# A hybrid decoder trunk: narrower kernel matrices in the recurrent branch, a new planned order, and a third fp32 weight tile per light chunk

## The chip, the cores and the metric

The kernel runs on one core of a Trainium2 chip. The metric is the device time of one execution in microseconds; three runs are taken and their median is compared. Beside them stands one profiled execution, whose trace gives every duration below.

## The reference, cut to what matters

256 tokens of width 1024 pass two layers. In each, one normalised input feeds sliding-window attention (8 query heads, 2 key heads) and a recurrent branch; both are normalised and go through one output matrix. Layer 0 ends in a dense gated block of width 3584, layer 1 in a mixture of 8 experts of the same width with the best 2 per token.

```
bb = f * b                                   # per group of 16 channels, 64 complex states
s  = associative_scan(a, einsum('blgc,gnc->blgn', u, bb))
y  = einsum(s_re, c_re) - einsum(s_im, c_im) + d_skip * u
y  = gelu(y);  y = y * sigmoid(y @ w_glu)
x  = x + mix @ w_o
x  = x + (silu(h @ wg) * (h @ wu)) @ wd      # dense, or top 2 of 8 experts
```

All arrays are float32.

## The kernel before

**Numbers.** A float32 weight tile of 128 x 1024 is loaded (`w`, 512 KB) and split into a rounded part `wh` (ScalarE) and the rest `wl` (VectorE), both float32r; the activation is split in the same way. A product takes three float32r matmuls (`mm3`: wh by xh, wl by xh, wh by xl), or one float32 matmul where a tile is used whole. Float32 matmuls show as two records each in the trace.

**Stages.** `mixer(0)`, `dense`, `mixer(1)`, `moe`. The dense block has 7 chunks of 512 hidden columns, 12 tiles each (4 gate, 4 up, 4 down), for two blocks of 128 tokens. The experts are sorted by the number of their rows and taken in the order of `TURNS`, a heavy one (up to 128 rows, places 0 to 3) and a light one (up to 64 rows, places 4 to 7) in turn, 7 chunks of 12 tiles each. A heavy chunk makes three matmuls per half tile. In a light chunk the stationary block holds the 64 high and the 64 low parts side by side, so that a half tile takes two matmuls (`both`), and the two halves of the result are added by a small matmul with `fold` after a copy `low` (`join`). A tile whose number is in `ENTIRE` isn't split: one float32 matmul per half tile reads it as it landed. That is tile 7, the last of the up half, in each of the 28 light chunks.

**The recurrent branch.** Four time steps are taken together. `prep` makes the input matrices G, the rotations E and the decay. `prep_out` makes the output matrices: H (`HB`, with zeros between the two groups of channels that share the partitions) and T, the direct path within four steps, from products of `BB` with `CB`, `DD` and `HB`. `ssm` runs two halves of 8 groups: input products into two banks, six VectorE instructions, two scans, the rotation back into `sr` and `si` (shifted by one step), then per group three products of 128 columns (with T, and with H for the real and the imaginary part), gelu, a turn, and the gated matrix.

**The order.** All instructions are recorded first. `Plan.order` simulates the five engines with its own cost of each instruction (`cost`), its own delay between engines (`lag`) and the number of buffers (44 of 4 KB per partition, 8 small ones, 8 banks), and always starts the ready instruction with the highest priority: its path to the end plus the entry of its stage in `BONUS`. Each engine then has its instructions in that order, as does SyncE's queue for the loads. The buffers are handed out in that order too: a load waits in SyncE's queue until the buffer that it takes has been read. `prep(1)` and `prep_out(1)` are recorded behind the dense block and may start after its first chunks.

Of the kernel before, what the change touches and what calls it, by code (L numbers as in the profile page):

```python
# [13 lines left out]
AF = mybir.ActivationFunctionType  # L14
# [15 lines left out]
TURNS = (0, 4, 1, 5, 2, 6, 3, 7)  # L30
GROUPS = {0: (0,), 1: (1,), 2: (2, 3), 4: LIGHT}

ENTIRE = (7,)
HEADS = [0, 4, 1, 5, 2, 6, 3, 7]
EPS = 1e-6
BIG = 1e30
# [111 lines left out]


class Plan:  # L150
    between, rate = 0.0027, 360e3

    def __init__(self):
        Plan.between, Plan.rate = 0.0027, 360e3
# [55 lines left out]
    @staticmethod  # L210
    def cost(eng, method, a, k):
        size = lambda v: int(np.prod(v.shape[1:]))
        if method == "registers":
            return 0.5
        if eng == "DMA":
            return int(np.prod(a[0].shape)) * 4 / Plan.rate + 0.01
        n = max(size(v) for v in a if isinstance(v, View))
        if eng == "PE":
            if method == "transpose":
                return 2 * size(a[2]) / 2400 + 0.001  # L220
            if a[2].buf.dtype == F32R:
# [226 lines left out]
class Kernel:  # L448
    NM = 44
    NH = 8  # L450
    gate_at = 6
    BONUS = {'qkv1': -5, 'att0': 43, 'att0s': 29, 'prep0': 5, 'us1': -15, 'xt0': 8, 'ssm1y': -83, 'ssm0g': 60, 'u0': -47, 'wo01': 87, 'qkv0': 2, 'hn': -49, 'route': -33, 'wo011': 54, 'att1s': -26, 'prepo1': -82, 'moe': -5, 'route1': -2, 'att0v': 10, 'rs': -22, 'wo11': 8, 'ssm0': 3, 'route0': 42, 'ssm1': 5, 'wo010': -5, 'att1v': 40, 'xt1': 12, 'us0': 5, 'gates': 5, 'prep1': 15, 'ssm1g': 20, 'att1': 2, 'wo10': 2, 'wo110': -2, 'u1': -2}
    QF = (0, 0)
    HOLD = (1, 2)
    LEAN = (14, 7)
# [344 lines left out]
    def prep_out(self, R):  # L800
# [5 lines left out]
        cr = R["bc"][:, 512:768].rearrange("p (g c) -> p g c", g=16)  # L806
        ci = R["bc"][:, 768:].rearrange("p (g c) -> p g c", g=16)
        dsk = P[0:32, 48:64]
        HB = [[self.M(f"HB{q}{g}") for g in range(2)] for q in range(2)]
        CB = self.M("CB").rearrange("p (r g h c) -> p r g h c", r=2, g=16, h=2)  # L810
        BB = self.M("BB").rearrange("p (r g h c) -> p r g h c", r=2, g=16, h=2)
        T = [self.M(f"T{g}") for g in range(2)]
        for t in HB[0] + HB[1] + T:
            nc.gpsimd.memset(t, 0.0)
        nc.gpsimd.memset(CB, 0.0)
        nc.gpsimd.memset(BB, 0.0)
        for h in range(2):
            ps = slice(64 * h, 64 * h + 64)
            act(CB[ps, 0, :, h, :], cr[ps], AF.Copy)
            act(CB[ps, 1, :, h, :], ci[ps], AF.Copy, scale=-1.0)  # L820
            for q in range(2):
                act(BB[ps, q, :, h, :], Gn[q][ps, :, 3, :], AF.Copy)
        pr = pf[:, 0].unsqueeze(3).to_broadcast([128, 16, 4, 16])
        pi = pf[:, 1].unsqueeze(3).to_broadcast([128, 16, 4, 16])
        c0 = cr.unsqueeze(2).to_broadcast([128, 16, 4, 16])
        c1 = ci.unsqueeze(2).to_broadcast([128, 16, 4, 16])
        for q, (x0, x1) in enumerate(((c0, c1), (c1, c0))):
# [7 lines left out]
            for g in range(2):  # L835
                v = HB[q][g].rearrange("p (g j h c) -> p g j h c", g=8, j=4, h=2)
                for h in range(2):
                    ps = slice(64 * h, 64 * h + 64)
                    act(v[ps, :, :, h, :], w0[ps, 8 * g:8 * g + 8], AF.Copy)
        R["H"] = HB  # L840
        DD = self.H("DD")[0:32].rearrange("p (g c) -> p g c", g=16)
        tt(DD, self.ident[0:32, 0:32].unsqueeze(1).to_broadcast([32, 16, 32]),
           dsk.unsqueeze(2).to_broadcast([32, 16, 32]), OP.mult)
        for b in range(4):
            bank = self.bank()
            g, i0 = b // 2, 4 * (b % 2)
            for k in range(4):
                gp = 4 * b + k
                o = (i0 + k) * 128
                c = k * 128  # L850
                l0, l1, r0, r1 = (x[:, q, gp].rearrange("p h c -> p (h c)") for x in (BB, CB) for q in range(2))
# [6 lines left out]
            src = bank[0:32].rearrange("p (k m) -> p k m", k=4)  # L858
            dst = T[g].rearrange("p (k m) -> p k m", k=8)
            for j in range(4):  # L860
                x, y = dst[32 * j:32 * j + 32, i0:i0 + 4, 32 * j:128], src[:, :, 0:128 - 32 * j]
                if j == 3:
                    nc.vector.tensor_copy(x, y)
                else:
                    act(x, y, AF.Copy)
        R["T"] = T


    def ssm(self, R, X, src, whole):
# [4 lines left out]
        for h in range(2):  # L874
# [9 lines left out]
            (a0, a1), (b0, b1), (sr, si) = (self.two(n) for n in ("sa", "sb", "s"))  # L884
            tt(a0, ec, zr, OP.mult)
            tt(b0, es, zi, OP.mult)
            tt(a0, a0, b0, OP.add)
# [7 lines left out]
            for x in (sr, si):  # L895
                nc.clear(x.rearrange("p (g k) -> p g k", g=8)[:, :, 0:1])
            tt(a0, ec, b0, OP.mult)
            tt(a1, es, b1, OP.mult)
            tt(late(sr), soon(a0), soon(a1), OP.subtract)
            tt(a0, ec, b1, OP.mult)  # L900
            tt(a1, es, b0, OP.mult)
# [5 lines left out]
            for b in range(2):  # L907
                Y = self.bank()
                for i in range(4):
# [5 lines left out]
                    nc.tensor.matmul(y, X[:, gp * 64:(gp + 1) * 64], R["T"][h][:, w], start=True, stop=False)  # L915
                    nc.tensor.matmul(y, sr[:, m], R["H"][0][h][:, w], start=False, stop=False)
                    nc.tensor.matmul(y, si[:, m], R["H"][1][h][:, w], start=False, stop=True)
                act(Yg[0:64, 512 * b:512 * b + 512].rearrange("p (j g c) -> p g j c", j=4, g=4),
                    Y[0:64, :].rearrange("p (g j c) -> p g j c", g=4, j=4), AF.Gelu_apprx_tanh)
# [810 lines left out]
```

## Time and profile before

| | |
|---|---|
| median of 3 runs (lowest to highest) | 1419.39 us (1418.64 to 1421.01) |
| profiled execution, its span | 1417.69 us, 1415.9 us |
| mean granted TensorE clock | 0.993 of 2.4 GHz |
| busy: TensorE, weight loads, VectorE, ScalarE | 1374.0, 1073.1, 1204.1, 998.9 us |
| read from memory | 420.10 MB, of it 672 tiles of 512 KB of the experts |

Busy times are shares of engines, not of the path: matmuls are pipelined and the end of each is modelled, so a TensorE that is always busy may still pause for fractions of a microsecond. The distance from one start to the next tells what an instruction costs in a row of its like. Windows give the busy time of each engine in a stretch, the granted clock, and the share and rate of the DMA engines.

### The profile page before, as it was taken

How to read it: one execution, taken by the hardware profiler on the slowest of the kernel's cores; microseconds unless marked ns; L12 is line 12 of the kernel's file. 1: busy time of each engine (PE TensorE's matmuls, PEld its weight loads, DVE VectorE, ACT ScalarE, POOL GpSimd, SP SyncE). 2: the span in 40 equal slices, each digit the busy share in tenths (PEclk: the TensorE clock that was granted, in tenths of full speed). 3: DMA queues.
4: the chain of work that ended last, by engine and by line, in shares of the span. 5: the costliest groups of instructions: out<-in, count | busy, mean ns of one | idle time of the engine just before them, and what ended most of it. 6: DMA issues, size and time to landing. Idle time of an engine off the chain costs nothing.

```text
span 1415.9 us, 20663 instructions
## 1 busy us (share of the span) xinstructions
PE 1374.0 (97%) x6550; PEld 1073.1 (76%) x6550; DVE 1204.1 (85%) x1642; ACT 998.9 (71%) x1314; POOL 25.5 (2%) x44
## 2 busy tenths in 40 slices
PE   7999999999999999999999999999999999999996
PEld 4888888888888878877678876778887667887654
DVE  8889985554685699999989889989989999998987
ACT  5486754444527387799787788878779778787775
POOL 3000110000000000000000000000000000000000
PEclk9999999999999999999999999999999999999999
DMA  6357155555546759689999999999999999999993
GB/s 220 101 172 252 46 161 177 192 193 162 168 141 240 296 192 360 251 334 397 359 375 371 394 388 406 395 352 370 390 387 393 395 408 372 385 381 400 409 408 146
DMA packets 116899, 422.57 MB, mean 298 GB/s; under 512 B 13360, under 2 KB 13872, under 8 KB 116784
## 3 DMA queue, kind: packets, MB, share of 16 engines
q1 hardware_dynamic: 116784, 421.20, 79.5%
q8 instruction: 53, 0.87, 0.2%
q14 instruction: 62, 0.51, 0.1%
HBM read 420.10 MB, written 1.05 MB: 297 GB/s over the span
## 4 chain that ended last, share of the span: by engine, by line
PE 85%; DVE 6%; DMA 3%; issue 3%; ACT 2%; SPq 0%; DVEq 0%; ACTq 0%
PE bank L445 85%; DVE wl L445 4%; DMA w<-in_moe_dram 3%; ACT wh L445 2%; DMA w<-in_win_u_dram 1%; DVE X L445 1%; ACT st L445 0%; SPq L445 0%; DVE ht L445 0%; DVE htl L445 0%; ACT xh L445 0%; DVE psm L445 0%; DVE xl L445 0%; ACT L445 0%; DVE yl L445 0%
## 5 line engine op out<-in xcount | busy, mean ns | idle before, releaser
L445 DVE TENSOR_TENSOR wl<-w,wh 128x1024 fp32r<-128x1024 f32 x758 | 882.7, 1215 | 86.8 <-ACT wh L445 54.2
L445 ACT ACTIVATE wh<-w 128x1024 fp32r<-128x1024 f32 x758 | 749.3, 1052 | 80.3 <-DMA w<-in_dense_dram 29.5
L445 PE MATMUL bank<-wh,xh 128*128 128x512 f32 x448 | 174.8, 396 | 2.8 <-DVE ht L445 1.9
L445 PE MATMUL bank<-wl,xh 128*128 128x512 f32 x448 | 171.7, 394 | 0.8 <-DVE wl L445 0.8
L445 PE MATMUL bank<-wh,xl 128*128 128x512 f32 x448 | 171.5, 393 | 0.1
L445 PE MATMUL bank<-wl,lx 128*128 128x512 f32 x392 | 159.0, 407 | 8.3 <-DVE wl L445 7.9
L445 PE MATMUL bank<-wh,lx 128*128 128x512 f32 x392 | 152.4, 398 | 8.6 <-DVE ht L445 4.7
L445 PE MATMUL bank<-wh,hth 128*128 128x512 f32 x336 | 115.5, 399 | 0.0
L445 PE MATMUL bank<-wh,htl 128*128 128x512 f32 x336 | 114.5, 399 | 0.0
L445 PE MATMUL bank<-wl,hth 128*128 128x512 f32 x336 | 114.4, 396 | 0.0
L445 PEld LDWEIGHTS bank<-wl,lx 128*128 128x128 f32 x392 | 74.5, 190 | 41.8 <-DVE wl L445 26.6
L445 PEld LDWEIGHTS bank<-wh,xh 128*128 128x128 f32 x448 | 84.0, 188 | 22.0 <-ACT wh L445 2.9
L445 PEld LDWEIGHTS bank<-wl,xh 128*128 128x128 f32 x448 | 84.4, 188 | 20.8 <-DVE wl L445 3.2
L445 PEld LDWEIGHTS bank<-wh,xl 128*128 128x128 f32 x448 | 84.0, 189 | 17.7 <-DVE xl L445 0.5
L445 PEld LDWEIGHTS bank<-wh,lx 128*128 128x128 f32 x392 | 74.3, 190 | 26.3 <-ACT wh L445 6.5
L445 PE MATMUL bank<-wh,hh 128*128 128x512 f32 (+1 forms) x288 | 91.5, 385 | 0.4
L445 PE MATMUL bank<-wl,hh 128*128 128x512 f32 (+1 forms) x288 | 90.1, 381 | 0.0
L445 PE MATMUL bank<-wh,hl 128*128 128x512 f32 (+1 forms) x288 | 90.0, 380 | 0.0
L445 PE MATMUL bank<-wh,ht 128*128 128x512 f32 x224 | 89.0, 431 | 0.6 <-ACT wh L445 0.6
L445 PE MATMUL bank<-wl,ht 128*128 128x512 f32 x224 | 84.6, 406 | 2.0 <-DVE wl L445 2.0
L445 PEld LDWEIGHTS bank<-wh,htl 128*128 128x128 f32 x336 | 62.8, 188 | 14.4 <-issue 1.2
L445 PEld LDWEIGHTS bank<-wh,hth 128*128 128x128 f32 x336 | 62.5, 188 | 14.0 <-issue 0.5
(308 smaller groups left out, 1732.1 us busy)
## 6 DMA issues: line engine op xcount, KB each, us to landing
w<-in_moe_dram SPq DMA_DIRECT2D x672, 512.0 KB, 6.3
w<-in_dense_dram SPq DMA_DIRECT2D x84, 512.0 KB, 4.3
w<-in_wo_dram SPq DMA_DIRECT2D x16, 512.0 KB, 4.4
w<-in_win_u_dram SPq DMA_DIRECT2D x8, 512.0 KB, 5.1
w<-in_win_q_dram SPq DMA_DIRECT2D x8, 512.0 KB, 7.6
w<-in_win_kv_dram SPq DMA_DIRECT2D x4, 512.0 KB, 3.6
w<-in_wglu_dram SPq DMA_DIRECT2D x4, 512.0 KB, 3.6
X<-in_x_dram SPq DMA_DIRECT2D x2, 512.0 KB, 4.2
```

The lines of the kernel that those rows point to most:

```text
L445: getattr(engines[o["eng"]], o["method"])(*map(real, o["a"]), **{n: real(v) for n, v in o["k"].items()})
```

## The change

It has three parts. First, the matrices of the recurrent branch lose their zero blocks: the products that make T have 16 and 48 columns in place of 32 and 96, D is added by VectorE, the two channels of a pair are put apart by a factor per partition (`hm`) in the copy into T, and `ssm` keeps the state of each group with its real part above its imaginary part, so that two products of 64 columns take the place of two of 128. Second, the planner's costs, delay and bonuses are other numbers; bonuses may now also be given by stage and engine. Third, tile 3, the last of the gate half, is used whole in light chunks as tile 7 is.

```
-ENTIRE = (7,)
+ENTIRE = (3, 7)
...
 class Plan:
-    between, rate = 0.0027, 360e3
+    between, rate = 0.0135, 360e3
...
         if eng == "ACT":
-            return 0.05 + n * 0.000876 + (0.06 if any(isinstance(v, View) for v in k.values()) else 0)
+            more = 0.1 if any(isinstance(v, View) for v in k.values()) and a[1].buf.kind != "ps" else 0
+            return 0.05 + n * 0.000876 + more + (0.09 if "accum_out" in k else 0)
...
+        if method == "tensor_tensor_scan":
+            return 0.07 + n * 0.00204
...
-        return 0.0 if e == f == "PE" else LAT[e] + (0.13 if f == "PE" and e != "DMA" else 0.0)
+        return 0.0 if e == f == "PE" else LAT[e] + (0.03 if f == "PE" and e != "DMA" else 0.0)
...
-            prio[i] += self.bonus.get(o["tag"], 0.0)
+            prio[i] += self.bonus.get(o["tag"], 0.0) + self.bonus.get(f"{o['tag']}/{o['eng']}", 0.0)
...
-        HB = [[self.M(f"HB{q}{g}") for g in range(2)] for q in range(2)]
-        CB = self.M("CB").rearrange("p (r g h c) -> p r g h c", r=2, g=16, h=2)
+        HS = [self.M(f"HS{b}") for b in range(2)]
...
-        for t in HB[0] + HB[1] + T:
+        for t in T:
             nc.gpsimd.memset(t, 0.0)
-        nc.gpsimd.memset(CB, 0.0)
...
-            act(CB[ps, 0, :, h, :], cr[ps], AF.Copy)
-            act(CB[ps, 1, :, h, :], ci[ps], AF.Copy, scale=-1.0)
...
+        nc.vector.tensor_reduce(hm, eye, AX.X, OP.add)
+        tt(both, eye[:, 0], eye[:, 1], OP.add)
+        tt(DD, both.unsqueeze(1).to_broadcast([32, 16, 16]), dsk.unsqueeze(2).to_broadcast([32, 16, 16]), OP.mult)
+        act(cn, ci, AF.Copy, scale=-1.0)
...
-                    act(v[ps, :, :, h, :], w0[ps, 8 * g:8 * g + 8], AF.Copy)
+                    act(v[64 * q:64 * q + 64, :, h], w0[64 * h:64 * h + 64, 8 * b:8 * b + 8].rearrange("p g j c -> p g (j c)"), AF.Copy)
...
-                mm(bank[0:32, c:c + 32], l0, r0, start=True, stop=False)
-                mm(bank[0:32, c:c + 32], l1, r1, start=False, stop=False)
-                mm(bank[0:32, c:c + 32], self.ident[0:32, 0:32], DD[:, gp, :], start=False, stop=True)
-                mm(bank[0:32, c + 32:c + 128], l0, HB[0][g][:, o:o + 96], start=True, stop=False)
-                mm(bank[0:32, c + 32:c + 128], l1, HB[1][g][:, o:o + 96], start=False, stop=True)
+                mm(bank[0:32, o:o + 16], l0, cr[:, gp], start=True, stop=False)
+                mm(bank[0:32, o:o + 16], l1, cn[:, gp], start=False, stop=True)
+                late = [x[:, gp, 0:3].rearrange("p j c -> p (j c)") for x in Hn]
+                mm(bank[0:32, o + 16:o + 64], l0, late[0], start=True, stop=False)
+                mm(bank[0:32, o + 16:o + 64], l1, late[1], start=False, stop=True)
...
+            tt(src[:, :, 0], src[:, :, 0], DD[:, 8 * b:8 * b + 8], OP.add)
...
+                    if j == 3:
+                        ts(x, y, hm[:, h:h + 1], None, OP.mult)
+                    else:
+                        act(x, y, AF.Copy, scale=hm[:, h:h + 1])
...
-            tt(late(sr), soon(a0), soon(a1), OP.subtract)
...
-            tt(late(si), soon(a0), soon(a1), OP.add)
+            for q, (b2, b3, op) in enumerate(((b0, b1, OP.subtract), (b1, b0, OP.add))):
+                tt(a0, ec, b2, OP.mult)
+                tt(a1, es, b3, OP.mult)
+                for g in range(2):
+                    ps = slice(64 * g, 64 * g + 64)
+                    tt(late(ss[g][64 * q:64 * q + 64]), soon(a0[ps]), soon(a1[ps]), op)
...
-                    nc.tensor.matmul(y, sr[:, m], R["H"][0][h][:, w], start=False, stop=False)
-                    nc.tensor.matmul(y, si[:, m], R["H"][1][h][:, w], start=False, stop=True)
+                    for g in range(2):
+                        c = slice(64 * g, 64 * g + 64)
+                        nc.tensor.matmul(y[:, c], ss[g][:, m], R["H"][h][:, 128 * k + 64 * g:128 * k + 64 * g + 64], start=False, stop=True, skip_group_check=True)
```

`BONUS` had 35 entries, by stage; it has 103 now, by stage and by stage and engine, most of them other numbers (`'qkv0': 225` where it was 2, `'ssm1': 143` where it was 5, `'att1s': 80` where it was -26).

## Rows read from the trace of the kernel before

**Rows 1.** Chain that ended last, in order of time: start us, us, what.
```profile
21.06 43.76 PE bank L445 x310
...
86.14 152.87 PE bank L445 x748
...
342.44 108.96 PE bank L445 x759
...
513.82 139.31 PE bank L445 x635
```

**Rows 2.** Windows: us, busy of PE, PEld, DVE, ACT, POOL, clock, DMA, GB/s.
```profile
25.00:50.00 25.00, 25.00 (x125) 15.38 (x124) 23.31 (x65) 18.75 (x30) 1.11 (x3) 1.00 0.17 55
475.00:500.00 25.00, 22.93 (x132) 20.08 (x131) 15.57 (x83) 9.80 (x19) 0.00 (x0) 0.86 0.59 228
750.00:800.00 50.00, 50.00 (x228) 41.00 (x227) 45.48 (x45) 37.56 (x43) 0.00 (x0) 1.00 0.99 374
850.00:946.00 96.00, 91.13 (x392) 67.06 (x391) 94.71 (x104) 82.98 (x106) 0.00 (x0) 0.98 1.01 396
1060.00:1170.00 110.00, 103.80 (x420) 74.31 (x420) 103.74 (x106) 89.06 (x108) 0.00 (x0) 0.98 1.02 399
```

**Rows 3.** Windows, ScalarE's turn copies hth (heavy), ht (light) alone; first, last of seven.
```profile
960.00:962.00 2.00, 0.59 (x1) 1.00 0.98 381
...
1060.00:1062.00 2.00, 0.60 (x1) 1.00 1.03 406
...
1076.00:1078.00 2.00, 0.38 (x1) 1.00 1.06 385
...
1170.00:1172.00 2.00, 0.39 (x1) 1.00 1.03 412
```

**Rows 4.** Timeline of TensorE in prep_out of layer 1: start us, us, instruction.
```profile
413.98 0.24 PE L445 MATMUL bank<-DD,K 32*32 32x32 f32 x2
...
418.40 0.68 PE L445 MATMUL bank<-HB,BB 128*32 128x96 f32 x6
418.91 0.23 PE L445 MATMUL bank<-CB,BB 128*32 128x32 f32 x2
...
419.66 0.29 PE L445 MATMUL bank<-CB,BB 128*32 128x32 f32 x4
419.88 0.24 PE L445 MATMUL bank<-DD,K 32*32 32x32 f32 x2
```

**Rows 5.** Timeline of TensorE in ssm of layer 1, input and output products.
```profile
388.55 7.25 PE L445 MATMUL bank<-Xs,G 128*128 128x64 f32 x64
395.61 0.48 PE L445 MATMUL bank<-wl,hh 128*128 128x512 f32 x1
...
433.82 1.04 PE L445 MATMUL bank<-T,Xs 128*64 128x128 f32 x8
434.69 0.38 PE L445 MATMUL bank<-HB,s 128*64 128x128 f32 x2
```

**Rows 6.** Groups by form, whole span: instruction, count, busy us, mean ns, idle before.
```profile
L445 DVE TENSOR_TENSOR wl<-w,wh 128x1024 fp32r<-128x1024 f32 x758 | 882.7, 1215 | 86.8 <-ACT wh L445 54.2 <-PE bank L445 29.1 <-DMA w<-in_moe_dram 1.5
L445 ACT ACTIVATE wh<-w 128x1024 fp32r<-128x1024 f32 x758 | 749.3, 1052 | 80.3 <-DMA w<-in_dense_dram 29.5 <-PE bank L445 29.2 <-DVE wl L445 19.5
...
L445 DVE TENSOR_TENSOR s<-sa 128x504 f32<-128x504 f32 x8 | 5.3, 674 | 0.1
```

**Rows 7.** Timeline of TensorE in a light chunk: split tiles and one whole tile.
```profile
1343.19 0.40 PE L445 MATMUL bank<-wh,lx 128*128 128x512 f32 x1
1343.43 0.39 PE L445 MATMUL bank<-wl,lx 128*128 128x512 f32 x1
...
1345.43 1.88 PE L445 MATMUL bank<-w,lx 128*128 128x512 f32 x4
1346.74 0.80 PE L445 MATMUL bank<-wh,ht 128*128 128x512 f32 x1
1347.38 0.40 PE L445 MATMUL bank<-wl,ht 128*128 128x512 f32 x1
```

**Rows 8.** Timeline of TensorE, the first expert's first product.
```profile
494.10 0.48 PE L445 MATMUL bank<-wh,xh 128*128 128x512 f32 x1
```

More of the change, by code (lines that the diff above doesn't have):

```diff
@@ L150 @@
 class Plan:
-    between, rate = 0.0027, 360e3
+    between, rate = 0.0135, 360e3
     def __init__(self):
-        Plan.between, Plan.rate = 0.0027, 360e3
+        Plan.between, Plan.rate = 0.0135, 360e3
         self.scratch = bacc.Bacc("TRN2", target_bir_lowering=False, num_devices=1)
@@ L818, in prep_out @@
             ps = slice(64 * h, 64 * h + 64)
-            act(CB[ps, 0, :, h, :], cr[ps], AF.Copy)
-            act(CB[ps, 1, :, h, :], ci[ps], AF.Copy, scale=-1.0)
             for q in range(2):
                 act(BB[ps, q, :, h, :], Gn[q][ps, :, 3, :], AF.Copy)
+        small = self.H("DD")
+        hm, both = small[0:32, 256:258], small[0:32, 272:288]
+        eye = self.ident[0:32, 0:32].rearrange("p (h c) -> p h c", h=2)
+        nc.vector.tensor_reduce(hm, eye, AX.X, OP.add)
+        DD = small[0:32, 0:256].rearrange("p (g c) -> p g c", g=16)
+        tt(both, eye[:, 0], eye[:, 1], OP.add)
+        tt(DD, both.unsqueeze(1).to_broadcast([32, 16, 16]), dsk.unsqueeze(2).to_broadcast([32, 16, 16]), OP.mult)
+        cn = self.H("cn")[:, 0:256].rearrange("p (g c) -> p g c", g=16)
+        act(cn, ci, AF.Copy, scale=-1.0)
         pr = pf[:, 0].unsqueeze(3).to_broadcast([128, 16, 4, 16])
@@ L826, in prep_out @@
         c1 = ci.unsqueeze(2).to_broadcast([128, 16, 4, 16])
+        Hn = []
         for q, (x0, x1) in enumerate(((c0, c1), (c1, c0))):
@@ L834, in prep_out @@
                 stt(w0, w0, -1.0, w1, OP.mult, OP.subtract)
-            for g in range(2):
-                v = HB[q][g].rearrange("p (g j h c) -> p g j h c", g=8, j=4, h=2)
+            Hn.append(w0)
+            for b in range(2):
+                v = HS[b].rearrange("p (g h m) -> p g h m", g=8, h=2)
                 for h in range(2):
-                    ps = slice(64 * h, 64 * h + 64)
-                    act(v[ps, :, :, h, :], w0[ps, 8 * g:8 * g + 8], AF.Copy)
-        R["H"] = HB
-        DD = self.H("DD")[0:32].rearrange("p (g c) -> p g c", g=16)
@@ new lines, in prep_out @@
+                    act(v[64 * q:64 * q + 64, :, h], w0[64 * h:64 * h + 64, 8 * b:8 * b + 8].rearrange("p g j c -> p g (j c)"), AF.Copy)
+        R["H"] = HS
+        for b in range(2):
+            bank = self.bank()
+            for k in range(8):
+                gp = 8 * b + k
+                l0, l1 = (BB[:, q, gp].rearrange("p h c -> p (h c)") for q in range(2))
+                mm = nc.tensor.matmul
+                o = 64 * k
+                mm(bank[0:32, o:o + 16], l0, cr[:, gp], start=True, stop=False)
[3 more added lines that the diff above has]
+                mm(bank[0:32, o + 16:o + 64], l1, late[1], start=False, stop=True)
+            src = bank[0:32].rearrange("p (k j c) -> p k j c", k=8, j=4)
+            tt(src[:, :, 0], src[:, :, 0], DD[:, 8 * b:8 * b + 8], OP.add)
+            dst = T[b].rearrange("p (k h j c) -> p k h j c", k=8, j=4, h=2)
+            for j in range(4):
+                for h in range(2):
+                    x, y = dst[32 * j:32 * j + 32, :, h, j:4], src[:, :, 0:4 - j]
+                    if j == 3:
+                        ts(x, y, hm[:, h:h + 1], None, OP.mult)
+                    else:
+                        act(x, y, AF.Copy, scale=hm[:, h:h + 1])
@@ L883, in ssm @@
             ec, es, dec = Ec[:, c], Es[:, c], R["dec"][:, c]
-            (a0, a1), (b0, b1), (sr, si) = (self.two(n) for n in ("sa", "sb", "s"))
+            (a0, a1), (b0, b1), ss = (self.two(n) for n in ("sa", "sb", "s"))
             tt(a0, ec, zr, OP.mult)
@@ L894, in ssm @@
             soon = lambda x: x.rearrange("p (g k) -> p g k", g=8)[:, :, 0:63]
-            for x in (sr, si):
+            for x in ss:
                 nc.clear(x.rearrange("p (g k) -> p g k", g=8)[:, :, 0:1])
-            tt(a0, ec, b0, OP.mult)
-            tt(a1, es, b1, OP.mult)
-            tt(late(sr), soon(a0), soon(a1), OP.subtract)
-            tt(a0, ec, b1, OP.mult)
-            tt(a1, es, b0, OP.mult)
-            tt(late(si), soon(a0), soon(a1), OP.add)
+            for q, (b2, b3, op) in enumerate(((b0, b1, OP.subtract), (b1, b0, OP.add))):
[4 more added lines that the diff above has]
+                    tt(late(ss[g][64 * q:64 * q + 64]), soon(a0[ps]), soon(a1[ps]), op)
             self.plan.tag = tag + "y"
@@ L914, in ssm @@
                     y = Y[0:64, 128 * i:128 * i + 128]
-                    nc.tensor.matmul(y, X[:, gp * 64:(gp + 1) * 64], R["T"][h][:, w], start=True, stop=False)
-                    nc.tensor.matmul(y, sr[:, m], R["H"][0][h][:, w], start=False, stop=False)
-                    nc.tensor.matmul(y, si[:, m], R["H"][1][h][:, w], start=False, stop=True)
-                act(Yg[0:64, 512 * b:512 * b + 512].rearrange("p (j g c) -> p g j c", j=4, g=4),
-                    Y[0:64, :].rearrange("p (g j c) -> p g j c", g=4, j=4), AF.Gelu_apprx_tanh)
+                    nc.tensor.matmul(y, X[:, gp * 64:(gp + 1) * 64], R["T"][h][:, w], start=True, stop=False, skip_group_check=True)
+                    for g in range(2):
+                        c = slice(64 * g, 64 * g + 64)
+                        nc.tensor.matmul(y[:, c], ss[g][:, m], R["H"][h][:, 128 * k + 64 * g:128 * k + 64 * g + 64], start=False, stop=True, skip_group_check=True)
+                act(Yg[0:64, 512 * b:512 * b + 512].rearrange("p (j g c) -> p g j c", j=4, g=8),
+                    Y[0:64, :].rearrange("p (g j c) -> p g j c", g=8, j=4), AF.Gelu_apprx_tanh)
                 for j in range(4):
```

18 lines of the change are left out of this document (1 added, 17 removed).

## The prediction

> **What bounds the kernel now.** I read the chain of waits first. From 21 us on it is TensorE almost without a break: 310 instructions in one piece of 43.76 us, and later pieces of 109 and 139 us [rows 1]. So layer 0, the dense block and layer 1 up to the router cost what TensorE's queue costs, and an instruction less there shortens the end by its own distance to the next. The windows say the same: 25.00 us busy of 25 in the mixer of layer 0 [rows 2]. A busy TensorE can still hold pauses, because the ends of its instructions are modelled; so below I price an instruction by the distance between starts, never by its duration.
>
> The one thin place before the experts is the router, 475 to 500 us: TensorE is busy 22.93 us of 25 at a mean granted clock of 0.86, which is a mix of its two levels, 2.4 and 1.2 GHz, after gaps in which it waited [rows 2].
>
> The experts split in two kinds. In a heavy one (750 to 800 us) TensorE is full, VectorE is at 45.48 of 50, and the DMA moves 374 GB/s; a chunk of 12 tiles takes (1060 - 960) / 6 = 16.7 us from one turn of the hidden block to the next [rows 2, 3]. In a light one the two are nearer to each other: (1170 - 1076) / 6 = 15.7 us per chunk [rows 3], VectorE busy 94.71 of 96 us in the second light expert and 103.74 of 110 in the third, DMA share 1.01 and 1.02 at 396 and 399 GB/s [rows 2]. So in the light experts VectorE and the loads stand side by side as the bound, and TensorE is behind them.
>
> **The change, part by part: the recurrent branch's kernel matrices (`prep_out`).** Per group of channels the kernel before issues two products of 32 columns with CB, one with DD, and two of 96 columns with HB; each fp32 product shows as two records. Nine DD pairs lie between 413.98 and 419.88 us in layer 1 with nothing but this work between, so one group costs 5.90 / 8 = 0.74 us [rows 4]. The change leaves two products of 16 columns and two of 48, eight records. Four records of 32 columns take 419.88 - 419.66 = 0.22 us, 0.055 each, and six of 96 columns 418.91 - 418.40 = 0.51 us, 0.085 each [rows 4]. The new widths are not in the trace. The lower end is 0.055 for all eight, 0.44 us; the upper end puts the 48-column ones at 0.085, 0.56 us. I take 0.44, because 48 columns are nearer to 32 than to 96. That saves 0.30 us per group (0.18 at the other end), with 16 groups in each of 2 layers 9.6 us (5.8). All of it stands on TensorE's path [rows 1].
>
> **The outputs (`ssm`).** Per group the kernel before has three products of 128 columns. Eight such records take 434.69 - 433.82 = 0.87 us, 0.109 each, so a group costs 0.65 us [rows 5]. The change keeps the one with T and replaces the other two by two of 64 columns, with stationary blocks of 64 columns as before. Such a record is not in the trace. Below it lies the 0.055 of rows 4 (and half of 0.109 is the same); above it lies a record that also moves 64 columns but loads a stationary block of 128: 64 of them in 395.61 - 388.55 = 7.06 us, 0.110 each [rows 5]. I take 0.07, nearer the low end because both sizes are half of a row known at 0.11. A group then costs 0.22 + 4 x 0.07 = 0.50 us and saves 0.15; 32 groups save 5 us. The ends are 6.9 us (0.055) and nothing (0.110).
>
> The trace's 0.110 for a stationary block of 128 columns whatever the moving width is what the Trainium skill gives as a rule (TensorE: Matmul & The Clock Gate, section LDWEIGHTS): loading takes the number of columns divided by 1.2 GHz, 107 ns for 128 and 53 ns for 64. By that rule this term would be 6.9 us in place of 5, an estimate from the page; no run here shows the 64 x 64 case.
>
> **What the same step adds elsewhere.** The shifted state goes into a block with real part above imaginary part, so VectorE writes it in half as many partitions with twice as many instructions: 8 more in all. They process as many elements per partition, so I price each at the present 674 ns: 5.4 us [rows 6]. The work hides it as long as TensorE has attention products and loads to do while the scan runs; VectorE is busy 23.31 of 25 us early in layer 0 [rows 2], so the cover is thin, and if it goes the price is up to 5.4 us. I cost it at nothing and keep 5.4 for the range. ScalarE has as many copies of H and T as before (T's now with a factor per partition) and four CB copies less per layer for one of cn; it has 6 us free in that window [rows 2], nothing. POOL loses five fills per layer that nobody waits for, nothing.
>
> **The new order.** Costs in the planner and its bonuses change, so every engine's queue is rearranged, loads and buffers with it. What it can give is what TensorE stands idle now: about 2 us at the router in rows 2 and the start before 21 us. What it can take is a queue in which TensorE waits for ScalarE or VectorE. I take zero, with 4 us on either side.
>
> **The third tile whole.** In each of 28 light chunks one more tile goes to TensorE as it lands. Removed: one split on ScalarE (1052 ns) and one on VectorE (1215 ns) [rows 6]. TensorE pays: the four records of a whole tile begin at 1345.43, the next instruction runs on to 1347.38, less its own 0.23, so 1.72 us; a split tile is four products 0.23 apart, 0.93 us [rows 7]. That is 0.79 us more per chunk, 22 us over 28 chunks. TensorE's own work in a light chunk is 11 x 0.93 + 1.72 and some 0.9 for folding and turning, 12.9 us, so 13.6 us afterwards: still below 15.7, and I cost it at nothing. If the cover is gone it costs up to 22 us. VectorE's part falls from 15.7 x 94.71 / 96 = 15.5 to 14.3 us. Late next are the loads: 12 tiles of 0.524 MB at 399 GB/s are 15.8 us, and the loads reach 410 in the same light experts [rows 3], 15.35 us. I take the chunk from 15.7 to 15.35: 28 x 0.35 = 9.8 us. Tiles already landed when a light expert starts could let it go below the load rate for a while; the floor is VectorE's 14.3, 28 x 1.4 = 39 us, which would need 440 GB/s throughout. So this term runs from -39 to +22.
>
> **Sum.** -9.6 - 5 - 9.8 = -24.4 us. The profiled execution took 1417.7 us, its span 1415.9; it lies 1.7 us below the median of the three runs, 1419.4. So 1419.4 - 24.4 = **1395 us**.
>
> **Rivals.**
> *The loads are the bound of the light experts* (1404 us). Then relief on VectorE gives nothing, and only the 14.6 us on TensorE before the experts are left. For it: a DMA share of 1.02 [rows 2]. Against it: 374 GB/s in a heavy expert [rows 2], so the loads wait there for buffers and could run ahead if a light expert gave them back sooner.
> The Trainium skill leans to this rival (DMA: Bandwidth & Descriptors, section Where 436 GB/s comes from): for transfers from HBM the memory's share of about 358 GB/s binds, below the fabric's 435. The trace disagrees with the 358, since 110 us ran at 399; by 435, a chunk would take 14.5 us, an estimate from the page.
>
> *The light experts fall to VectorE's new pace for a part of the time* (1381 us): 0.35 becomes 0.85 us per chunk, 24 us, because heavy experts fill the buffers ahead and light ones eat the stock. For it: 98.7% of VectorE in the second light expert [rows 2]. Against it: a stock of buffers is worth only a few tiles.
>
> *TensorE becomes late in the light experts* (1427 us, slower). Its place is the first chunks after a heavy expert, where it still works off what lies before it, and then every chunk whose fp32 tile stands ahead of ready work in its queue: the 22 us come in full, less 14.6 in the mixers. It decides once TensorE's pauses in a light chunk, now 15.7 - 12.9 = 2.8 us, fall at the wrong place, so that 0.79 us of work finds no pause: from two chunks in three on it eats the mixers' gain (14.6 / 0.79 = 18 of 28). Against it: 2.8 us is three times what is added.
>
> *It does not do what it says*: narrow products cost as much as wide ones and the new order puts VectorE's 5.4 us on the path; the light experts stay. Then 5.8 - 5.4, no change, 1419 us.
>
> **How the numbers follow.** Forecast 0.45, loads bound 0.25, VectorE's pace 0.15, TensorE late 0.10, no effect 0.05. The forecast and the first two rivals are faster; with the last two split, faster by over 0.2% (2.8 us, about what a measurement of this kernel can tell from no change) has 0.85, same 0.05, slower 0.10. The range 1379 to 1415 takes in the first three with their unknown prices and leaves out TensorE late and most of no effect; below it lies a part of VectorE's pace.
>
> **What would show it.** Steps one and two: the first product of the first heavy expert starts 12 to 17 us before the present 494 us [rows 8], and a group in `prep_out` takes 0.44 us. If it starts where it did, the order or the DVE additions ate the gain. Step three: turns of the hidden block in light experts 15.3 to 15.4 us apart, VectorE near 90% there, heavy chunks still 16.7. Light chunks of 16 us or more with TensorE's pauses gone would be TensorE late; 15.7 unchanged with the DMA share at 1.02 would be the loads. What would make the prediction wrong altogether is a pause of TensorE of ten or more us in a mixer, which the rearranged queues could hold and the profile of before cannot show.

## The result: slower by 11.9 us

The changed kernel takes 1430.96 us (median of 4 runs, 1429.89 to 1433.23), the kernel before 1419.07 (1418.64 to 1421.01): ratio 1.0088, 95% interval 1.0071 to 1.0105. The forecast was 1395, its range 1379 to 1415. The profiled execution has a span of 1431.4 us, 15.5 more than before, at a mean granted clock of 0.983. Of these 15.5 us some 3.6 come from the choice of the two executions: the one before lies 1.4 us below its median, the changed one 2.3 above.

Two halves make up the 15.5 us. The first product of the first expert starts 8.2 us later than before [rows 8], and from there to the end it takes 929.1 us where it took 921.8, 7.3 us more. The line of the tile `xh` in the changed kernel:

```profile
L448 PE MATMUL bank<-wh,xh x1: 481/481/481, 502.3 to 502.3; 128*128 128x512 f32 x1
```

**Each product became as cheap as forecast, or cheaper.** TensorE's timeline in layer 1 of the changed kernel: the 16 groups of `prep_out` stand in a row, and further down are the new 64-column products.

```profile
419.30 0.24 PE L448 MATMUL bank<-bc,BB 128*32 128x16 f32 x2
...
423.90 0.34 PE L448 MATMUL bank<-ht,BB 128*32 128x48 f32 x4
428.61 1.09 PE L448 MATMUL bank<-T,Xs 128*64 128x128 f32 x4 [4.37 <-ACT T L448]
...
438.83 0.63 PE L448 MATMUL bank<-HS,s 128*64 128x64 f32 x8
439.29 0.39 PE L448 MATMUL bank<-T,Xs 128*64 128x128 f32 x2
```

Sixteen groups from 419.30 to about 424.07 (0.17 us are taken for the last four records, as for others of their kind) are 0.30 us each (forecast 0.44, before 0.74 [rows 4]). Eight records with 64 stationary and 64 moving columns take 439.29 - 438.83 = 0.46 us, 0.0575 each (forecast 0.07). So TensorE's work fell by some 32 x 0.44 + 32 x 0.20 = 20.5 us, where 14.6 had been forecast. The third row shows where it went: the next product waits 4.37 us for ScalarE's copies into T.

**TensorE pauses in the mixers, and then runs at the low clock.** Windows of the changed kernel, columns as in rows 2; the first and fourth answer to the first two of [rows 2], the last three to the rest:

```profile
25.00:50.00 25.00, 20.53 (x81) 10.98 (x80) 20.94 (x74) 17.78 (x30) 0.95 (x1) 0.86 0.07 22
75.00:100.00 25.00, 19.51 (x108) 14.22 (x105) 24.29 (x46) 18.53 (x54) 0.00 (x0) 0.85 0.39 126
425.00:450.00 25.00, 20.76 (x173) 19.79 (x173) 20.00 (x45) 20.67 (x37) 0.26 (x1) 0.80 0.68 229
475.00:500.00 25.00, 23.15 (x121) 20.27 (x120) 17.66 (x91) 5.38 (x11) 0.00 (x0) 0.83 0.84 312
750.00:800.00 50.00, 49.15 (x224) 40.15 (x223) 48.37 (x49) 39.16 (x45) 0.00 (x0) 1.00 0.99 372
850.00:946.00 96.00, 96.00 (x404) 68.61 (x403) 85.45 (x95) 74.80 (x95) 0.00 (x0) 1.00 1.01 395
1060.00:1170.00 110.00, 107.68 (x425) 73.69 (x424) 97.00 (x101) 79.06 (x95) 0.00 (x0) 1.00 1.02 400
```

The second and third of these windows in the kernel before:

```profile
75.00:100.00 25.00, 24.82 (x193) 20.47 (x192) 20.77 (x49) 19.85 (x55) 0.00 (x0) 1.00 0.52 176
425.00:450.00 25.00, 25.00 (x183) 20.01 (x182) 14.48 (x30) 19.81 (x56) 0.00 (x0) 1.00 0.62 218
```

The stretch from 25 us had TensorE busy 25.00 of 25 at 1.00; now it is 20.53 at 0.86. The waits of TensorE that the profile lists from 20 to 500 us add up to 19 us, before to 4.

**The third tile helped two light experts and not the other two.** In the second light expert (850 to 946 us) VectorE falls from 94.71 to 85.45 us of 96, TensorE rises from 91.13 to 96.00, and the rate stays at 395 GB/s. The turn copies of [rows 3] in the changed kernel, first and last of seven: heavy (`hth`), then light (`ht`) in the second and in the third light expert:

```profile
964.00:966.00 2.00, 0.60 (x1) 1.00 1.00 406
...
1066.00:1068.00 2.00, 0.31 (x1) 1.00 0.96 332
...
861.00:863.00 2.00, 0.39 (x1) 1.00 1.02 406
...
953.00:955.00 2.00, 0.39 (x1) 1.00 0.98 383
...
1081.00:1082.00 1.00, 0.38 (x1) 1.00 1.01 406
...
1180.00:1181.00 1.00, 0.38 (x1) 1.00 0.96 361
```

That is (953 - 861) / 6 = 15.3 us per light chunk in the second light expert, as forecast (15.35), but (1180 - 1081) / 6 = 16.5 in the third, where [rows 3] gave 15.7; and (1066 - 964) / 6 = 17.0 per heavy chunk, before 16.7. By the starts of the copies the four light experts take 15.2, 15.3, 16.6 and 16.9 us per chunk, before 15.7, 15.9, 15.8 and 16.2. In the last two TensorE still has pauses:

```profile
1081.00:1181.00 100.00, 96.49 (x374) 64.02 (x372) 87.03 (x92) 70.62 (x87) 0.00 (x0) 1.00 1.02 401
1311.00:1412.00 101.00, 94.03 (x353) 61.67 (x351) 81.53 (x83) 70.68 (x87) 0.00 (x0) 0.98 0.93 363
```

**A pause in the mixer.** TensorE's timeline at the first pause, then the end of another:

```profile
31.62 0.38 PE L448 MATMUL bank<-bc,BB 128*32 128x16 f32 x4 [4.47 <-issue]
31.93 9.98 PE L448 MATMUL bank<-w,h 128*128 128x512 f32 x16
41.75 0.27 PE L448 MATMUL bank<-K,GB 128*128 128x128 f32 x1
41.86 3.60 PE L448 MATMUL bank<-w,h 128*128 128x512 f32 x8
45.30 0.93 PE L448 MATMUL bank<-K,GB 128*128 128x128 f32 x7
...
94.92 0.73 PE L448 MATMUL bank<-wh,ml 128*128 128x512 f32 x2 [2.18 <-DVE ml L448]
```

Two tiny products with BB stand in the queue ahead of q products that are ready. BB comes late, for VectorE does the H products first. Before, the same place had a shorter pause; and the clock behind the new one:

```profile
21.06 0.49 PE L445 MATMUL bank<-CB,BB 128*32 128x32 f32 x8 [2.40 <-ACT BB L445]
```
```profile
34.00:36.00 2.00, 2.00 (x4) 0.81 (x3) 2.00 (x6) 1.95 (x4) 0.00 (x0) 0.50 0.00 0
```

After 4.47 us of waiting, 16 records take 41.75 - 31.93 = 9.82 us, 0.61 each, where the next eight take 45.30 - 41.86 = 3.44 us, 0.43 each. So the pause costs 2.9 us more after it has ended, in a stretch at the lower of the two levels (1.2 GHz, a granted clock of 0.50).

### The profile page after: what moved, and what is told of

Its sections match the earlier page's. It is cut to its first block, busy times and chain, and to the rows that moved or that the text cites. A ratio compares the mean times of both kernels' runs of the same rounds, so it can differ in the third digit from the quotient of the medians.

```text
span 1431.4 us, 20435 instructions
## 1 busy us (share of the span) xinstructions
PE 1380.9 (96%) x6486; PEld 1063.9 (74%) x6486; DVE 1181.5 (83%) x1630; ACT 973.7 (68%) x1280; POOL 16.1 (1%) x34
## 4 chain that ended last, share of the span: by engine, by line
PE 85%; DVE 7%; ACT 4%; issue 2%; DMA 2%; SPq 0%; DVEq 0%; ACTq 0%
PE bank L448 85%; DVE wl L448 3%; DMA w<-in_moe_dram 1%; ACT wh L448 1%; ACT T L448 1%; DVE sa L448 1%; ACT st L448 1%; DVE X L448 1%; DVE s L448 1%; DVE sb L448 0%; DMA X<-in_x_dram 0%; ACT HS L448 0%; ACT xh L448 0%; DVE ht L448 0%; DVE htl L448 0%
## 5 line engine op out<-in xcount | busy, mean ns | idle before, releaser
L448 DVE TENSOR_TENSOR wl<-w,wh 128x1024 fp32r<-128x1024 f32 x730 | 853.3, 1217 | 122.4 <-ACT wh L448 94.0
L448 ACT ACTIVATE wh<-w 128x1024 fp32r<-128x1024 f32 x730 | 722.2, 1052 | 93.8 <-DMA w<-in_dense_dram 33.5
L448 PE MATMUL bank<-wl,lx 128*128 128x512 f32 x336 | 146.8, 437 | 5.7 <-DVE wl L448 5.4
L448 PE MATMUL bank<-wh,lx 128*128 128x512 f32 x336 | 136.1, 411 | 3.1 <-DVE ht L448 2.5
L448 PE MATMUL bank<-w,lx 128*128 128x512 f32 x224 | 107.4, 592 | 0.0
L448 ACT ACTIVATE low<-bank 128x512 fp32r<-128x512 f32 x56 | 33.4, 597 | 85.0 <-PE bank L448 84.9
L448 PEld LDWEIGHTS bank<-wl,lx 128*128 128x128 f32 x336 | 63.7, 190 | 36.1 <-DVE wl L448 19.2
L448 PEld LDWEIGHTS bank<-wh,lx 128*128 128x128 f32 x336 | 63.8, 190 | 25.9 <-issue 9.2
```

Source lines behind the costliest of these rows:

```text
L448: getattr(engines[o["eng"]], o["method"])(*map(real, o["a"]), **{n: real(v) for n, v in o["k"].items()})
```

## Experiments

The three parts were first taken apart, then the engines' loads changed one at a time. The table gathers what the profiles show: the start of the first expert's first product, and from there to the end of the span. Times are medians beside the kernel before on the same chip.

| kernel | time, us | ratio to before (95%) | first expert at | from there to the end |
|---|---|---|---|---|
| before | 1417 to 1421 | | 494.1 | 921.8 |
| changed | 1430.96 | 1.0071 to 1.0105 | 502.3 | 929.1 |
| e1 tile 3 alone | 1418.33 | 0.9976 to 1.0000 | 494.4 | 919.9 |
| e2 branch alone | 1447.94 | 1.0180 to 1.0214 | 524.3 | 921.5 |
| e3 order alone | 1445.23 | 1.0150 to 1.0199 | 521.4 | 921.9 |
| e4 branch and tile | 1448.76 | 1.0184 to 1.0229 | 528.4 | 922.4 |
| e5 branch and order | 1423.32 | 1.0015 to 1.0034 | 501.3 | 919.4 |
| e8 a load less | 1422.54 | 1.0004 to 1.0035 | 498.1 | 926.2 |
| e9 a load less, tile 3 | 1413.74 | 0.9948 to 0.9975 | 498.2 | 914.7 |
| e10 less TensorE | | | 488.8 | |
| e11 more VectorE | 1420.71 | 1.0012 to 1.0043 | 496.0 | 921.5 |
| e12 both | | | 493.6 | |
| e13 branch, own bonuses | 1415.16 | 0.9953 to 0.9982 | 494.2 | 917.3 |
| e14 old branch, own bonuses | 1418.63 | 0.9975 to 1.0011 | 499.8 | 920.9 |
| e15 new costs, other bonuses | 1426.59 | 1.0031 to 1.0058 | 502.8 | 923.0 |
| e16 e13 with tile 3 | 1417.11 | 0.9966 to 0.9992 | 494.9 | 918.9 |

**How far one profile can be read.** Kernels that differ only in the experts agree on the start of the first expert within 1.0 us (before and e1, the changed one and e5, e8 and e9, e13 and e16); only e2 and e4 are 4.1 apart. So smaller differences in this column say little. One difference has nothing to do with the edits. In the profiles of e3, e8, e9, e10 and e14 a small VectorE instruction at 7 us lasts until POOL's fills end, and the first product of layer 0 starts 3 us late. Before, then e10:

```profile
6.74 0.44 DVE L445 TENSOR_SCALAR nsink<-prm 128x8 f32<-128x8 f32 x1
9.01 5.36 PE L445 MATMUL bank<-w,h 128*128 128x512 f32 x12
```
```profile
7.05 4.58 DVE L458 TENSOR_SCALAR nsink<-prm 128x8 f32<-128x8 f32 x1
9.77 1.84 POOL L458 MEMSET T<- 128x1024 f32 x2
12.00 2.93 PE L458 MATMUL bank<-w,h 128*128 128x512 f32 x3 [2.38 <-DVE h L458]
```

The instruction ends at 7.05 + 4.58 = 11.63 us, the fills at 9.77 + 1.84 = 11.61. In the other four profiles of the old branch (before, e1, e11, e12) it takes at most 0.53 us beside the same fills, so this is chance, and the shift stays: e8 and e9, in which VectorE and ScalarE have the instructions of before in the same order up to there, start the first expert at 498.1 and 498.2. The new branch has five fills less; POOL is done at about 7.2 us, and none of its seven profiles shows the wait.

**The parts alone.** e1 is the kernel before with the first of these lines, e5 the changed kernel without it; e2 has the branch under the old planner, e3 the new costs, delay and bonuses with the old branch, e4 is e2 with the tile.

```
-ENTIRE = (7,)
+ENTIRE = (3, 7)
```

e1: 

> The kernel before with tile 3 of each light chunk whole as well, nothing else. The theory (the new order of the mixers costs the time): light chunks hardly move, 1410 to 1419 us, turns of the hidden block 15.4 to 15.7 us apart. Rival (TensorE late in the light experts, which grew by 7 us between the first expert's first product and the end): 1424 to 1430 us, light chunks at 16 us or more.

e2: 

> The kernel before with the recurrent branch without zero blocks, under the planner's costs and bonuses of before, tile 3 split. The theory (the branch saves about 21 us of TensorE by the trace after: 0.29 for 0.74 us per group, 0.44 for 0.65 us per group; the order lost them): 1398 to 1408 us, the dense block's statistics at 125 to 130 us for 133.9. Rival (the branch itself is late: T waits for VectorE's addition and ScalarE's twelve scaled copies, whatever the order): 1415 to 1430 us with the same pause of over 4 us before the first product with T.

e3: 

> The kernel before under the changed costs, delay and bonuses alone. The theory (the order is what costs): 1435 to 1455 us, with pauses of TensorE in both mixers and their clock below 0.9 there. Rival (the order is right for the new branch and only the branch or the tile is at fault): within 5 us of before, 1414 to 1424 us. The bonuses were chosen with the new branch, so a slow run here is weaker evidence than a fast one.

e5: 

> The changed kernel with tile 3 split again. The theory (order): 1427 to 1436 us, since the mixers keep their pauses. Rival (tile): 1417 to 1423 us, light chunks back at 15.7 us.

e4: 

> The kernel before with the new branch and tile 3 whole, costs and bonuses as before: what the change is without its order. The new branch under the old order took 1447.9 us. If a whole tile 3 in itself delays TensorE in light chunks, this is 7 to 10 us above that, 1455 to 1458, as it was under the new order (1423.3 to 1431.0). If its price is a matter of how the order happens to interleave the light experts, it is anything within 10 us of 1448; with the loads as the bound and no accident, 1446 to 1448.

Measured: branch alone +28 us, order alone +25, both together about +3.5. Under the new order the branch gains 1445.2 - 1423.3 = 22 us, about what it takes from TensorE; under the old one it loses 28, which lies above both ranges of e2's expectation. Neither part has a price of its own: an order fits one branch. The tile, read from the first expert to the end, gives -1.9 (e1 against before), +0.9 (e4 against e2) and +9.7 (changed against e5). Within one kernel it differs from expert to expert (us per light chunk, from the starts of the turn copies):

| kernel | 1st | 2nd | 3rd | 4th light expert |
|---|---|---|---|---|
| before | 15.7 | 15.9 | 15.8 | 16.2 |
| e1, e4, e16: tile 3, old costs | 14.8 | 15.9 | 16.1 | 16.0 to 16.1 |
| e5: new costs, tile split | 14.8 | 16.8 | 15.7 | 16.2 |
| changed: new costs, tile 3 | 15.2 | 15.3 | 16.6 | 16.9 |
| e8: a load less | 15.7 | 16.9 | 15.9 | 16.2 |
| e9: a load less, tile 3 | 14.8 | 16.1 | 14.3 | 14.9 |

e1, e4 and e16 agree within 0.05 us, so they are one order of the experts, read three times. With tile 3 split and all loads the experts take 917 to 923 us in every kernel of the table, wherever they start; so what the mixers lose arrives at the end in full.

**Do the loads bind a light chunk, or VectorE?** In e8 tile 7 isn't loaded, in e9 tile 3 is whole besides.

```
-        w = self.M("w")
+        w = self.raw = self.M("w")
...
-                w = self.load(src[4 * q + n], 4 * q + n in ENTIRE)
+                w = (self.raw, None) if 4 * q + n == 7 else self.load(src[4 * q + n], 4 * q + n in ENTIRE)
```

e8: 

> The kernel before, with one load less in each of the 28 light chunks: tile 7 is not loaded, its products read the float32 tile 6 that is there already. So that half of the up projection is not the reference's; TensorE, VectorE and ScalarE do what they did. 14.7 MB of 420 are not read. Theory (the loads alone bind a light chunk): a light chunk is 12 tiles of loading, so 11/12 of 15.7 to 16.3 us, 1.3 us less, and the time is 28 x 1.3 = 36 us lower, about 1384. Rival (VectorE, 98.7% busy in the second light expert, binds as well): the chunk stays within 0.3 us of 15.7 to 16.3 and the time is 1411 to 1419, with the rate of the loads in light experts down from 400 to some 370 GB/s.

e9: 

> The kernel before with tile 3 whole and again without the load of tile 7 in light chunks (its products read tile 6). Both suspects are relieved: a light chunk has 10 splits in place of 11 and 11 loads in place of 12. If loads and VectorE stand side by side as the bound, each relief alone gives next to nothing (tile 3 whole alone gave 1.6 us) and both together 20 to 36 us: 1383 to 1399. If the loads alone bind, this is no faster than the kernel that only leaves out the load. If TensorE is late (0.79 us more per light chunk), it is slower than that kernel by up to 22 us.

The same stretch of the last light expert, first before, then e8, then e9 (columns as in rows 2):

```profile
1310.00:1390.00 80.00, 73.61 (x280) 46.46 (x280) 73.56 (x75) 62.11 (x75) 0.00 (x0) 1.00 1.02 408
```
```profile
1310.00:1390.00 80.00, 73.99 (x299) 53.82 (x297) 76.97 (x77) 68.75 (x84) 0.00 (x0) 0.98 0.94 363
```
```profile
1310.00:1390.00 80.00, 80.00 (x321) 56.26 (x320) 72.14 (x73) 65.46 (x81) 0.00 (x0) 1.00 0.90 344
```

A twelfth of the loads less: the rate falls to 363 GB/s, VectorE goes to 76.97 of 80 and the time doesn't fall; three of the four light experts keep the pace of before. VectorE relieved too: TensorE is at 80.00 of 80, the rate at 344, and the whole kernel gains 0.4%, not the 20 to 36 us that were expected. The tile, with a load less, gives 914.7 - 926.2 = -11.5 us, and the gain of e9 over e1 stands in the third and fourth light expert. The loads alone do not bind, nor does VectorE alone (e1), and once both are relieved TensorE is full. The edits also change the planned order of the experts, which these runs do not separate from the relief.

**What shorter products are worth in the mixers.** Here every queue keeps the old order instruction by instruction; only sizes change where the instructions are issued.

```
+                if r == "DD":
+                    continue
...
+                if l == "s":
+                    c = slice(64 * (r[:3] == "HB1"), 64 * (r[:3] == "HB1") + 64)
+                    a[0], a[2] = a[0][:, c], a[2][:, c]
...
```
```
+            if o["eng"] == "DVE" and o["method"] == "tensor_tensor" and o["a"][0].buf.name == "s":
+                for h in range(2):
+                    nc.vector.tensor_tensor(*(x.get()[64 * h:64 * h + 64] if isinstance(x, View) else x for x in map(lambda y: (real(y), y)[1], o["a"])), **o["k"])
+                continue
```

e10 has the first edit, e11 the second, e12 both. Without D and a part of the state's output the router chooses otherwise, so e10 and e12 end in the loop for overfull experts (4338 and 4346 us) and are read up to the first expert only.

e10: 

> The kernel before with every queue in its own order, instruction by instruction, but less work in TensorE's: the 32 DD products are not issued (D is left out of T), and each of the two HB products of a group in ssm covers 64 of its 128 columns (a part of the state's output is left out). By rows of the kernel before and after this takes 32 x (0.74 - 4 x 0.055 - 4 x 0.085 = 0.18) = 5.8 us and 64 x 2 x (0.109 - 0.0575) = 6.6 us from TensorE, 12.4 us in all, with nothing else changed. Theory (TensorE's work is the path in the mixers, as the forecast had it, and only the new order's pauses ate the gain): 12 us less, about 1407. Rival (VectorE and ScalarE stand right behind TensorE in the mixers, so shorter products become pauses): under 5 us less, 1414 to 1419, with TensorE under 25.00 us of 25 in windows where it was full.

e11: 

> The kernel before with every queue in its own order, and one thing more: each of the 8 shifted state writes (128 partitions x 504) is issued as two of 64 partitions, as the changed kernel does, so VectorE has 8 instructions of about 0.68 us more. The result is the same. The forecast costed this at nothing, with 5.4 us if the cover is gone. Theory (VectorE is right behind TensorE in the mixers): 4 us or more are paid, 1422 to 1425. Rival (hidden, as forecast): 1418 to 1420, TensorE full in the same windows.

e12: 

> Both edits of the two kernels before this one in one: 12.4 us less on TensorE, 5.4 us more on VectorE, every queue in its old order; D and a part of the state's output are left out. If TensorE's work is the path and VectorE hidden: 1407. If both are paid: 12.4 - 5.4 = 7 us less, 1412. If VectorE's and ScalarE's chain is what remains once TensorE has less: no gain or a loss, 1418 to 1425, which would mean that the recurrent branch's saving on TensorE cannot be cashed by any order that keeps VectorE's work.

Windows of the kernel before, then e10, e11 and e12:

```profile
50.00:75.00 25.00, 25.00 (x235) 22.18 (x234) 21.67 (x50) 9.89 (x21) 0.15 (x2) 1.00 0.48 148
400.00:425.00 25.00, 25.00 (x254) 21.85 (x252) 22.18 (x47) 8.74 (x18) 0.95 (x1) 1.00 0.51 169
```
```profile
50.00:75.00 25.00, 23.79 (x220) 21.94 (x219) 21.80 (x48) 8.81 (x20) 0.15 (x2) 0.86 0.44 131
400.00:425.00 25.00, 21.62 (x236) 19.12 (x235) 23.83 (x50) 12.99 (x26) 0.95 (x1) 1.00 0.62 201
```
```profile
50.00:75.00 25.00, 24.42 (x232) 21.70 (x231) 22.65 (x50) 9.88 (x21) 0.15 (x2) 1.00 0.50 148
400.00:425.00 25.00, 24.66 (x248) 21.64 (x248) 24.36 (x49) 6.58 (x16) 0.95 (x1) 1.00 0.43 143
```
```profile
50.00:75.00 25.00, 22.52 (x202) 20.64 (x200) 21.35 (x47) 8.97 (x21) 0.15 (x2) 0.86 0.47 144
400.00:425.00 25.00, 20.04 (x210) 18.72 (x208) 24.36 (x49) 8.90 (x19) 0.95 (x1) 0.86 0.52 168
```

12.4 us less on TensorE bring the first expert from 494.1 to 488.8, 5.3 us; but e10 has the late start and before has not. Against e8 and e9, whose start is as late, it is 9.3 us, three quarters of what was taken away. 5.4 us more on VectorE put the first expert back by 1.9 (e11); both together leave 0.5 (e12), and neither of these two has the late start. So behind the shorter products the same VectorE work costs some 8 to 9 us, more than its own length. The list of TensorE's waits from 20 to 500 us, in e10 and then in e12, names what comes late (engine and line, what it waited for: us in total, times, longest); before there was no row for T.

```profile
PE bank L458 <- ACT T L458: 3.4, 3, 1.7
```
```profile
PE bank L462 <- ACT T L462: 7.4, 3, 5.0
PE bank L462 <- ACT BB L462: 2.8, 1, 2.8
```

The chain from VectorE over ScalarE's copies to the products with T stands close behind TensorE.

**Would another order cash it?** e13 (new branch) and e14 (old) have the old costs, bonuses by stage and engine, and each a set of bonuses looked for with its own branch; e15 is e5 with other bonuses alone; e16 is e13 with tile 3 whole.

```
-            prio[i] += self.bonus.get(o["tag"], 0.0)
+            prio[i] += self.bonus.get(o["tag"], 0.0) + self.bonus.get(f"{o['tag']}/{o['eng']}", 0.0)
```

e13: 

> The new branch, tile 3 split, the planner's costs and delay as before, bonuses by stage and engine, and another set of them, looked for with this branch. Theory (TensorE, VectorE and ScalarE stand side by side in the mixers, so that no order cashes what the branch takes from TensorE): the long pauses go, and the time is that of the kernel before within 8 us, 1411 to 1427; the first expert's first product near 494 to 500 us. Rival (only the new order was bad; a fitting one cashes the branch's 21 us): 1395 to 1403, first expert product before 480 us.

e14: 

> The control to the kernel before this one: the old branch, tile 3 split, the old costs, and a set of bonuses looked for with the old branch in the same way. Theory: within 6 us of the new branch under its own bonuses, 1408 to 1425. Rival (the branch is worth its TensorE time once the order fits): this is 15 us or more slower than the new branch under its own.

e15: 

> The changed kernel with tile 3 split and the bonuses alone replaced by a set looked for with its own costs. The same kernel under the changed bonuses took 1423.3 us, with pauses of 4.5, 4.4 and about 6 us in the mixers. Theory (these pauses belong to that one order, and 8 us of the loss to them): 1412 to 1420, first expert product 3 to 6 us earlier than 501.3. Rival (they follow from the new costs): 1421 to 1427.

e16: 

> The new branch under its own bonuses, with tile 3 whole as the one difference. A fourth place to read the tile: it gave -1.6 us on the kernel before, +0.8 under the old order with the new branch and +7.6 under the changed order. Theory (no resource of a light chunk is free, so the tile moves VectorE's 1.2 us to TensorE's 0.8 and the rest is how the queues interleave): within 5 us of the same kernel with the tile split. Rival (TensorE late): 7 us or more slower.

e13 is the fastest whole kernel here, 15.8 us below the changed one and 0.3% below the one before, so the loss was not in the branch. But it is only 3.5 us faster than its control e14, not the 20.5 us that TensorE saves, and its first expert starts where it did before. (e14's profile has the late start, so the 499.8 of the table is some 3 us too high for a comparison.) The mixer of e13 in layer 0 shows why (window and wait):

```profile
50.00:75.00 25.00, 15.62 (x82) 12.16 (x81) 21.24 (x33) 7.02 (x15) 0.00 (x0) 0.80 0.42 146
```
```profile
PE bank L445 <- DVE wl L445: 8.0, 1, 8.0
```

TensorE waits 8.0 us for one `wl` that stands on VectorE behind the scans and the shifted states. One set of bonuses was tried per branch, so a better one is not ruled out. e15 fell to its rival: the list of its waits has the pause of 4.5 us and that of 4.4 at T under other bonuses too.

```profile
PE bank L448 <- ACT T L448: 4.8, 2, 4.4
PE bank L448 <- issue: 4.5, 1, 4.5
```

In e3, the old branch under the new costs, TensorE waits 5.3 us for the products with BB, and no kernel with the old costs waits there for more than 2.8. So the pause at BB goes with the new costs, under either branch and two sets of bonuses. e16 adds 1.6 us from the first expert on: the tile's fourth reading.

## Why the prediction was wrong

**The step that failed first** is "I cost it at nothing and keep 5.4 for the range", the VectorE additions. Alone they put the first expert back by 1.9 us (e11; 3.5 by the medians), so part was hidden. Behind the shorter products they take away nearly all that these gain: 9.3 us early without them (e10 against e8 and e9), 0.5 with them (e12 against before). The cover was the very work that the change removes, and VectorE at 23.31 of 25 [rows 2] was the row that warned. With both, the forecast's -14.6 us before the experts is about nothing. And e12 has not even all that was added: D's addition on VectorE is missing, and so is the factor in the copies into T, which the prediction took as unchanged (ScalarE's longest go from 0.59 to 0.68 us).

"All of it stands on TensorE's path [rows 1]" held for the greater part: with every queue in its order 9.3 of 12.4 us arrive. A chain that runs through TensorE without a break says that TensorE is the last to be late, not by how much the next one is earlier.

**"I take zero, with 4 us on either side"**, the new order. The first expert is 8.2 us late, where e12 has it 0.5 early: about 8.7 us for the order (e12 has not all of the branch's edits, neither its 20.5 us on TensorE nor the addition of D on VectorE), in pauses such as those at 31.62 and 428.61 us, with the low clock after them. The same branch, tile split, starts it at 501.3 in e5 and at 494.2 under e13's order, a direct reading of 7 us. The prediction named one pause of ten or more us as what would make it wrong, and gave it no chance of its own; what came were several, none above 4.5 us. e3 shows that an order can cost 25.

**"I take the chunk from 15.7 to 15.35"**, the third tile. -9.8 us was forecast; with all loads four readings give -1.9, +0.9, +1.6 and +9.7, the first three from one order of the experts. One expert's pace was taken for all 28 chunks, but it differs from expert to expert: with the tile whole it runs from 14.8 to 16.1 us in one order and from 15.2 to 16.9 in the other, while e10, e11 and e12, which keep the order of before, keep its paces within 0.25. The forecast came true in the first two light experts of the changed kernel and failed in the last two. The step behind it is that TensorE's 0.79 us per chunk is "still below 15.7, and I cost it at nothing". Its listed waits from the first expert on add up to 24 us before and 20 in e5; e1, e4 and e16 have 9 left, the changed kernel 15. So the added work, 22 us by the prediction's price, found cover in one order and too little in the other. Why is not settled. A suspect, which no run took away, is VectorE splitting four tiles ahead of a `ht` for which TensorE waits 2.49 us, in the fourth light expert:

```profile
1328.28 4.61 DVE L448 TENSOR_TENSOR wl<-w,wh 128x1024 fp32r<-128x1024 f32 x4
1332.82 0.41 DVE L448 TENSOR_TENSOR ht<-bank,ht 128x256 fp32r<-128x256 f32 x1
```
```profile
1333.37 0.47 PE L448 MATMUL bank<-wh,lx 128*128 128x512 f32 x1 [2.49 <-DVE ht L448]
```

The rival "TensorE becomes late" gave 1427 us, near the 1431 measured, but by luck: it was 22 us in the experts less 14.6 in the mixers, and what came were 7 us lost in the experts and 8 before them. Its sign, light chunks of 16 us or more without pauses of TensorE, is not there either: where the chunks are longer than 16 us, TensorE is at 96.49 of 100 and 94.03 of 101. The longest piece of the chain that ended last does run through TensorE:

```profile
765.72 325.63 PE bank L448 x1421
```

But it takes in the second light expert, which went faster. The rival "loads are the bound" had the tile at nothing, which three readings bear out, but by a wrong reason: e8.

**"POOL loses five fills per layer that nobody waits for, nothing"** is wrong for some executions: in five of nine profiles of the old branch VectorE waits for these fills' end, and the kernel is 3 us longer. This is a gain of the new branch that the sum does not have.

**Right** were the sizes of the products, on the low side. The 64 x 64 records at 0.0575 us put the `ssm` term at 6.4 us, nearer to the 6.9 that followed from the rule in the Trainium skill (TensorE: Matmul & The Clock Gate, section LDWEIGHTS) than to my 5. Right too was that an earlier first expert would come out at the end in full: with tile 3 split and all loads the rest takes 917 to 923 us from any start.

## What to carry to other kernels

Before an engine's saving is counted, take it away with every queue held in its order, and see what is late next: a full chain has no slack figure in it. Before two profiles are compared, look whether they start alike: a wait of 3 us in the first 12 nearly halved the reading of e10. A pace read on one stretch is not the pace of its like. Where the saving goes with more work on a second engine, the cover of that work shrinks by the saving, so the two must not be priced apart. And where a planner sets the order, a change of work and a change of order are one change: each alone cost 25 to 28 us here.

## What was not expected of the hardware

A share of the DMA engines of 1.02 is no proof that the loads bind: with a twelfth of them left out the light experts were no faster (e8). A pause of 4.5 us was followed by 16 records at 0.61 us on average in place of 0.43, so its price was well above its length (9.82 us, 16 x 0.43 = 6.9 at the later pace, so 2.9 us on top). And a VectorE instruction of 0.44 us took 4.58 when it lasted to the end of POOL's fills, in some executions of the same instructions and not in others; that the fills are the cause is inferred from the common end.
